# A fixed order of fill groups, smaller adds, and half of the embedding's projection computed ahead of q in an encoder layer

## The chip, the cores and the metric

One NeuronCore of a Trainium2 chip runs the whole kernel. The metric is the device time of one execution in microseconds (us). Three runs of the kernel before gave 1895.80, 1898.79 and 1899.89 us, median 1898.79.

## What is computed

One encoder layer on 256 tokens of width 2048, in float32: a feed-forward half, a mixer of attention heads, a second feed-forward half and a gated input embedding, each between two RMS norms.

```python
def _swiglu(u, w_gate, w_up, w_down):
    return (jax.nn.silu(u @ w_gate) * (u @ w_up)) @ w_down
...
        f = _swiglu(_rmsnorm(h, ffn1_pre_g[i]), ffn1_w_gate[i], ffn1_w_up[i], ffn1_w_down[i])
        h = h + 0.5 * _rmsnorm(f, ffn1_post_g[i])
        m = _mixer(_rmsnorm(h, mix_pre_g[i]), w_qkv[i], na_rpb[i], out_g[i], w_o[i])
        h = h + _rmsnorm(m, mix_post_g[i])
        f = _swiglu(_rmsnorm(h, ffn2_pre_g[i]), ffn2_w_gate[i], ffn2_w_up[i], ffn2_w_down[i])
        h = h + 0.5 * _rmsnorm(f, ffn2_post_g[i])
        g = jax.nn.sigmoid(_rmsnorm(h, ple_pre_g[i]) @ w_ple_gate[i])
        h = h + _rmsnorm(g * (p[i] @ w_ple_proj[i]), ple_post_g[i])
```

The hidden width is 5632, `p` is 256 x 256, `w_ple_proj` 256 x 2048. The embedding's projection `p @ w_ple_proj` depends on no other stage.

## The kernel before

**Numbers in two parts.** Every float32 operand is split into a high part (a cast to fp32r on ACT, ScalarE: `wh`, L81) and a low part (the rest, a subtraction on DVE, VectorE: `wl`, L82). A product of 128 rows is three matmuls of 512 columns: high by high, low by high, high by low (`mac`, L106 to L108; with `low_last`, L99 to L102, in another order). `split` works on two blocks of 128 weight rows at a time and has six buffers for each part, so the splits can run at most six pairs ahead of the matmuls that free them. Weights come by DMA in pieces of 512 KB (`raw`, four buffers, L72), or of 1 MB (`raw_b`, L192).

**The feed-forward half** (`swiglu`) runs over 11 blocks `nb` of 512 hidden columns. Block 0 is computed plainly. Blocks 1 to 10 take gate and up together (`pair_product`): with sums of the token tiles made beforehand (`s1` to `s4`) and sums of weights, seven products of eight row blocks replace eight. In blocks 2 to 10 they are, in order: a11 into bank g0 (copied to g1, L245); a12 into g0; s1 into u0 (copied to u1, L254); s4 into u0; s2 into g1 (copied out, L212); s3 into g1 (copied out, L212); a22 into g1. Each is 24 matmuls. The sums of weights are made in place: `add_rows` (L197) loads rows of w_up on the GpSimd queue with a DMA that adds them to what stands in the buffer, and `add` (L205) adds two buffers on DVE, in pieces of up to four row blocks. Block 1 (`apart`) has another order, in which six of the eight row blocks take part and two are multiplied plainly.

**Fills.** The down product of earlier blocks is cut into groups of 24 matmuls (`down`, for 512 output columns), and `fill()` runs the next one of the list `waiting` at certain places between the seven products. Blocks 3 to 10 have four groups, block 2 has three. The places in blocks 2 to 10 are: before a12; after s1 and the first `add`; after s2; after s3. A `None` in the list is an empty place. Output of a block, transposed (`tr`, L314), is made ready for its own down groups in the next block.

**Between the stages.** At the end of a half the last down groups are scaled and squared (L307, L479), and `residual` makes the factor of the post norm (L301 and L302 on DVE, a power on GpSimd, L303), updates h (L430), transposes it on TensorE (L314) and splits it for the next stage (L318, L320, L321). It is a generator that is run to its end by `list(res)`: after the first half come q and k of the first head group (`halves`), after the second half the embedding. There, all four blocks of 512 columns of `p @ w_ple_proj` are computed (`pp`: 48 matmuls, each block two row blocks, two token tiles, three matmuls), copied out of PSUM (L814) and kept in SBUF, in the place that the second half's sums had; then comes the product of h with `w_ple_gate` (`pg`).

**The order on each engine** is not that of the program text alone: the framework puts each instruction into its engine's queue by priority in program order among those that its own model holds ready. Each engine then works its queue in order.

Of the kernel before, what the change touches and what calls it, by code (L numbers as in the profile page):

```python
# [8 lines left out]
F32 = mybir.dt.float32  # L9
# [6 lines left out]
P = 128  # L16
D = 2048
S = 256
NT = S // P
# [4 lines left out]
NB = 512  # L24
# [10 lines left out]
def encoder_layer(ctx: ExitStack, tc: tile.TileContext, a: dict, out: bass.AP):  # L35
# [6 lines left out]
    nc = tc.nc  # L42
# [22 lines left out]
    def new_raw(name="raw"):  # L65
        return wpool.tile([P, 2, NB], F32, name=name, tag="raw", bufs=4)
# [27 lines left out]
    def mac(acc, xs, parts, first=False, last=False, low_last=False):  # L94


        if low_last:
            for i, ((xh, xl), (wh, wl)) in enumerate(zip(xs, parts)):
                nc.tensor.matmul(acc, xh, wh, start=first and i == 0, stop=False)  # L99
                nc.tensor.matmul(acc, xh, wl, start=False, stop=False)  # L100
            for i, ((xh, xl), (wh, wl)) in enumerate(zip(xs, parts)):
                nc.tensor.matmul(acc, xl, wh, start=False, stop=last and i == len(parts) - 1)  # L102
            return
        for i, ((xh, xl), (wh, wl)) in enumerate(zip(xs, parts)):
            lead, tail = first and i == 0, last and i == len(parts) - 1
            nc.tensor.matmul(acc, xh, wh, start=lead, stop=False, skip_group_check=True)  # L106
            nc.tensor.matmul(acc, xl, wh, start=False, stop=False, skip_group_check=True)  # L107
            nc.tensor.matmul(acc, xh, wl, start=False, stop=tail, skip_group_check=True)  # L108
# [61 lines left out]
    def pair_product(lhs, sums, wa, ca, wb, cb, fill, apart):  # L170

        def bank(name):
            return ps_acc.tile([P, NB], F32, name=f"pair_{name}", tag="acc")

        rq = RQ - 2 * apart
        rows1, rows2 = ([lhs[k] for k in ks[:rq]] for ks in ROWS)
        a11, a12, a22 = of_tile(rows1, 0), of_tile(rows2, 0), of_tile(rows2, 1)
        s1, s2, s3, s4 = (x[:rq] for x in sums)

        def spans(step):  # L180
            for k0, k1 in ((0, KB), (KB, rq)):
                for k in range(k0, k1, step):
                    yield k, min(k + step, k1)

        def weight_rows(w, j, c, k0, k1):
            r0 = ROWS[j][k0] * P
            return w[r0 : r0 + (k1 - k0) * P, c : c + NB].rearrange("(k p) n -> p k n", p=P)

        def blocks(w, j, c, i):
            raw = block_tile(i, [P, RQ, NB], "raw_b")  # L190
            for k0, k1 in spans(KB):
                raw_loads.append(nc.sync.dma_start(raw[:, k0:k1], weight_rows(w, j, c, k0, k1)))  # L192
            return raw

        def add_rows(raw, w, j, c):
            for k0, k1 in spans(2):
                nc.gpsimd.dma_start(raw[:, k0:k1], weight_rows(w, j, c, k0, k1), accum_op=ALU.add)  # L197

        def split_rows(raw):
            return sum((split(raw[:, k : min(k + 2, rq)]) for k in range(0, rq, 2)), [])  # L200

        def add(x, y):
            for k in range(0, rq, 4):
                j = slice(k, min(k + 4, rq))
                nc.vector.tensor_tensor(x[:, j], x[:, j], y[:, j], op=ALU.add)  # L205

        def combine(out_, x, y, op):
            nc.vector.tensor_tensor(out_, x, y, op=op)

        def copied(name, x):  # L210
            t = ffn_pool[0].tile([P, NB], F32, name=name, tag="part", bufs=3)
            nc.scalar.copy(t, x)  # L212
            return t


        def rest(w, c, accs_, i, first=False):
            ks = [x[i] for x in ROWS]
            raw = new_raw()
            rows_ = w[:, c : c + NB].rearrange("(k p) n -> p k n", p=P)
            raw_loads.append(nc.sync.dma_start(raw, rows_[:, ks[0] : ks[1] + 1 : ks[1] - ks[0]]))  # L220
            parts = split(raw)
            for t, acc in accs_:
                mac(acc, of_tile([lhs[k] for k in ks], t), parts, first=first)
        if apart:
            g0, g1, u0, u1 = (bank(x) for x in ("g0", "g1", "u0", "u1"))
            rest(wb, cb, [(1, u1), (0, u0)], RQ - 1, first=True)
            run_later()
            ra1, rb2 = blocks(wa, 0, ca, 0), blocks(wb, 1, cb, 1)
            mac(g1, a11, split_rows(ra1), first=True)
            p1 = copied("p1", g1)  # L230
            add_rows(ra1, wb, 0, cb)
            mac(u0, s4, split_rows(rb2))
            rest(wb, cb, [(1, u1), (0, u0)], RQ - 2)
            fill()
            mac(g0, s1, split_rows(ra1), first=True)
            p5 = copied("p5", g0)
            add(ra1, rb2)
            add_rows(rb2, wb, 0, cb)
            fill()
            ra2 = blocks(wa, 1, ca, 2)  # L240
        else:
            ra1 = blocks(wa, 0, ca, 0)
            g0, g1 = bank("g0"), bank("g1")
            mac(g0, a11, split_rows(ra1), first=True)
            nc.scalar.copy(g1, g0)  # L245
            add_rows(ra1, wb, 0, cb)
            run_later()
            ra2 = blocks(wa, 1, ca, 1)
            fill()
            mac(g0, a12, split_rows(ra2))  # L250
            rb2 = blocks(wb, 1, cb, 2)
            u0, u1 = bank("u0"), bank("u1")
            mac(u0, s1, split_rows(ra1), first=True)
            nc.scalar.copy(u1, u0)  # L254
            add(ra1, rb2)
            fill()
            mac(u0, s4, split_rows(rb2))
            add_rows(rb2, wb, 0, cb)
        mac(g1, s2, split_rows(ra1))
        t4 = ra1 if apart else ra2  # L260
        add(t4, ra2 if apart else ra1)
        u0_ = copied("u0_s", g1)
        if apart:
            combine(u0_, u0_, p5, ALU.subtract)
        combine(u0_, u0, u0_, ALU.subtract)
        fill()
        mac(g1, s3, split_rows(rb2))
        if apart:
            u1_ = p5
            combine(u1_, u1_, g1, ALU.subtract)  # L270
            combine(u1_, u1, u1_, ALU.add)
            mac(g0, a12, split_rows(ra2), first=True)
        else:
            u1_ = copied("u1_s", g1)
            combine(u1_, u1, u1_, ALU.subtract)
            fill()
        mac(g1, a22, split_rows(t4))
        if apart:
            rest(wa, ca, [(0, g0), (1, g1)], RQ - 2)
            rest(wa, ca, [(0, g0), (1, g1)], RQ - 1)  # L280
            combine(p1, g0, p1, ALU.add)
            g0 = p1
            fill()
        block_order[:] = [block_order[i] for i in ((1, 2, 0) if apart else (0, 2, 1))]
        return (g0, g1), (u0_, u1_)
# [172 lines left out]
    def swiglu(pool, f, ssf, res, blocks, rs, sums, w_gate, w_up, w_down, g_post, src):  # L458
# [37 lines left out]
        def downs(nb, b, hid):  # L496
            steps = [] if b not in left else [lambda x=left.pop(b): down(x[0], b, x[1], last=False)]
            return steps + [lambda first=not steps: down(nb, b, hid, first=first)]
# [5 lines left out]
        for nb in range(nbs):  # L504
# [48 lines left out]
            if nb < nbs - 1:  # L553
                now = (0, 1, 2) if nb == 0 else (3, 2) if nb % 2 else (0, 1)
                waiting = sum((downs(nb, b, hid) for b in now), [])
                left.update({b: (nb, hid) for b in range(D // NB) if b not in now})
        for b in (0, 1):
            down(left[b][0], b, left[b][1], last=False, **(dict(pool_=ps_acc, tag="acc") if b else {}))
# [15 lines left out]
                    scaled_out(b, t, acc[t], gp)  # L574


    with tc.tile_pool(name="ffn1", bufs=2) as pool:
        f = pool.tile([P, NT, D], F32, name="f", bufs=1)
        sums_pool[0] = pool
        ssf, u_blocks, u_rs = square_sums(), [], []  # L580
        res = residual(f, ssf, 2.0, u_blocks, u_rs, row_g[:, 1])
        swiglu(
            pool, f, ssf, res, x_blocks, None, [],
            a["ffn1_w_gate"], a["ffn1_w_up"], a["ffn1_w_down"], a["ffn1_post_g"],
            lambda t: a["x"][t * P : (t + 1) * P],
        )
        list(res)
    rs = u_rs

# [194 lines left out]
    mix.close()  # L784


    def embedding_rows():
        p_raw = new_raw("p_raw")
        nc.sync.dma_start(p_raw[:, :, :S], a["pT"].rearrange("(k p) s -> p k s", p=P))
        return split(p_raw[:, :, :S])  # L790

    with tc.tile_pool(name="ffn2", bufs=2) as pool:
        f = f_pool.tile([P, NT, D], F32, name="f")
        ssf, ple_blocks, ple_rs = square_sums(), [], []
# [11 lines left out]
    pp = []  # L806
    for n, pool_, tag in ((RQ, f_pool, "sums_l"), (NT * D // NB - RQ, pool, "pp")):
        y = pool_.tile([P, n, NB], F32, name="pp", tag=tag)
        pp += [y[:, i] for i in range(n)]
    for b in range(D // NB):  # L810
        acc = accs("pp")
        product(acc, p_rows, a["w_ple_proj"], 0, b * NB)
        for t in range(NT):
            nc.scalar.copy(pp[b * NT + t], acc[t])  # L814
# [102 lines left out]
```

## Time and profile before

| | |
|---|---|
| median of three runs | 1898.79 us |
| the profiled execution: its time | 1898.71 us |
| its span | 1896.9 us |
| mean granted TensorE clock | 0.997 |
| busy TensorE / weight loads | 98% / 81% |
| busy DVE / ACT / GpSimd | 80% / 66% / 12% |
| moved by DMA | 424.16 MB, mean 224 GB/s |

The profile is one execution. PE is TensorE, PEld its weight loads, POOL GpSimd, SP the queue that issues most DMAs. A row of a timeline gives start, duration, engine, line, operation, what is written and read, and in brackets the idle time of the engine before it with what ended it. A matmul's duration overlaps the next one's; the distance of starts is what it costs. A row of windows gives, for each engine, busy time and number of instructions in the stretch, then the granted clock, the DMA engines' busy share and their rate. A row of instructions by tile or line gives shortest, median and longest duration in ns, and first and last start.

The stages lie thus in the span: first feed-forward half to 695 us, mixer to 1100, second half to 1784, embedding to the end.

### The profile page before, as it was taken

Reading aid. Unit: us, or ns where it says so; the run is one execution under the profiler, and the core shown is the slowest. Engines: PE = TensorE matmul, PEld = TensorE weight load, DVE = VectorE, ACT = ScalarE, POOL = GpSimd, SP = SyncE. Lnnn points to the kernel's source line nnn. Section 1 sums busy time; section 2 is a strip of 40 time slices with the busy share of each in tenths; the row PEclk is TensorE's granted clock in tenths of the full one; section 3 lists DMA queues with packets and bytes.
Section 4 is the critical chain, followed back from the end, with each engine's and each line's share of the span. In section 5 each row is a group of like instructions: output and inputs, shape, how many; then the busy total and the mean of one; then the engine's idle time right before and its main releaser. Section 6 shows DMA issues by size and latency. Waiting matters only on the chain.

```text
span 1896.9 us, 23645 instructions
## 1 busy us (share of the span) xinstructions
PE 1866.1 (98%) x8492; PEld 1540.7 (81%) x8492; DVE 1525.7 (80%) x1554; ACT 1261.4 (66%) x1592; POOL 221.9 (12%) x189
## 2 busy tenths in 40 slices
PE   8999999999999999999999999999999999999997
PEld 6788888888888878888888888888888888888886
DVE  7898988889888875656665588889988898888765
ACT  7677867777776764544535466778677777767753
POOL 0111112121111100000000001111121111111110
PEclk9999999999999999999999999999999999999999
DMA  9989888898889756454454669898888988897563
GB/s 310 257 247 263 252 226 208 256 279 229 208 237 278 208 177 220 147 197 135 157 189 155 206 205 291 236 260 254 233 204 257 275 233 214 228 277 221 173 221 123
DMA packets 215477, 424.16 MB, mean 224 GB/s; under 512 B 11328, under 2 KB 14400, under 8 KB 214336
## 3 DMA queue, kind: packets, MB, share of 16 engines
q1 hardware_dynamic: 172640, 338.77, 52.5%
q0 software_dynamic: 42720, 83.90, 24.5%
q8 instruction: 66, 1.08, 0.2%
q14 instruction: 51, 0.42, 0.1%
HBM read 418.42 MB, written 4.19 MB: 223 GB/s over the span
## 4 chain that ended last, share of the span: by engine, by line
PE 75%; issue 10%; DMA 6%; DVE 5%; ACT 2%; POOL 1%; SPq 0%; DVEq 0%; POOLq 0%; ACTq 0%
PE pair_g L106 7%; PE pair_g L107 7%; PE pair_g L108 7%; PE down L108 7%; PE down L107 6%; PE down L106 6%; DMA raw_b<-in_ffn_w_up 4%; DVE wl L82 3%; PE pair_u L107 3%; PE pair_u L106 3%; PE pair_u L108 3%; PE v L107 2%; PE v L108 2%; PE v L106 2%; ACT wh L81 1%
## 5 line engine op out<-in xcount | busy, mean ns | idle before, releaser
L82 DVE TENSOR_TENSOR wl<-raw_b,wh 128x1024 fp32r<-128x1024 f32 x546 | 645.2, 1221 | 118.6 <-ACT wh L81 111.7
L81 ACT CAST wh<-raw_b 128x1024 fp32r<-128x1024 f32 x546 | 568.1, 1052 | 252.0 <-DMA raw_b<-in_ffn_w_up 114.6
L82 DVE TENSOR_TENSOR wl<-raw,wh 128x1024 fp32r<-128x1024 f32 (+1 forms) x381 | 459.7, 1219 | 141.4 <-ACT wh L81 129.4
L81 ACT CAST wh<-raw 128x1024 fp32r<-128x1024 f32 (+1 forms) x381 | 396.9, 1051 | 237.4 <-PE k L107 39.6
L197 POOL DMA_DIRECT2D raw_b<-in_ffn_w_up x156 | 190.7, 1274 | 1003.9 <-DVE wl L82 867.3
L108 PE MATMUL down<-wl,hid_h 128*128 128x512 f32 x640 | 251.0, 392 | 6.5 <-DVE wl L82 6.3
L106 PE MATMUL down<-wh,hid_h 128*128 128x512 f32 x640 | 251.0, 392 | 0.0
L107 PE MATMUL down<-wh,hid_l 128*128 128x512 f32 x640 | 249.2, 389 | 0.0
L108 PE MATMUL pair_g<-wl,u_h 128*128 128x512 f32 x484 | 188.3, 390 | 0.7 <-DVE wl L82 0.7
L106 PE MATMUL pair_g<-wh,u_h 128*128 128x512 f32 x484 | 188.5, 389 | 0.0
L107 PE MATMUL pair_g<-wh,u_l 128*128 128x512 f32 x484 | 188.3, 389 | 0.0
L205 DVE TENSOR_TENSOR raw_b<-raw_b 128x2048 f32<-128x2048 f32 x80 | 178.6, 2233 | 0.7
L108 PEld LDWEIGHTS down<-wl,hid_h 128*128 128x128 f32 x640 | 120.1, 188 | 37.5 <-DVE wl L82 12.9
L107 PEld LDWEIGHTS down<-wh,hid_l 128*128 128x128 f32 x640 | 120.2, 188 | 24.5
L106 PEld LDWEIGHTS down<-wh,hid_h 128*128 128x128 f32 x640 | 120.2, 188 | 23.8
L106 PE MATMUL pair_g<-wh,sums_h 128*128 128x512 f32 x324 | 126.2, 389 | 1.7 <-ACT u_s L212 1.7
L108 PE MATMUL pair_g<-wl,sums_h 128*128 128x512 f32 x324 | 126.1, 389 | 0.0
L107 PE MATMUL pair_g<-wh,sums_l 128*128 128x512 f32 x324 | 126.0, 389 | 0.0
L106 PE MATMUL pair_u<-wh,sums_h 128*128 128x512 f32 x300 | 116.7, 389 | 0.0
L107 PE MATMUL pair_u<-wh,sums_l 128*128 128x512 f32 x300 | 116.7, 389 | 0.0
L108 PE MATMUL pair_u<-wl,sums_h 128*128 128x512 f32 x300 | 116.7, 389 | 0.0
L108 PEld LDWEIGHTS pair_g<-wl,u_h 128*128 128x128 f32 x484 | 90.9, 188 | 20.0 <-DVE wl L82 1.2
(227 smaller groups left out, 2893.7 us busy)
## 6 DMA issues: line engine op xcount, KB each, us to landing
raw<-in_ffn_w_down SPq DMA_DIRECT2D x176, 512.0 KB, 9.0
raw_b<-in_ffn_w_up POOLq DMA_DIRECT2D x156, 512.0 KB, 10.1
raw_b<-in_ffn_w_gate SPq DMA_DIRECT2D x76, 1024.0 KB, 7.2
raw<-in_w_qkv SPq DMA_DIRECT2D x96, 512.0 KB, 4.8
raw_b<-in_ffn_w_up SPq DMA_DIRECT2D x38, 1024.0 KB, 7.4
raw<-in_w_o SPq DMA_DIRECT2D x32, 512.0 KB, 4.9
raw<-in_w_ple_gate SPq DMA_DIRECT2D x32, 512.0 KB, 5.1
raw<-in_ffn_w_up SPq DMA_DIRECT2D x20, 512.0 KB, 4.2
```

What stands on the lines that cost most here:

```text
L81: nc.scalar.copy(wh[:, :n], raw),
L82: nc.vector.tensor_tensor(wl[:, :n], raw, wh[:, :n].bitcast(F32), op=ALU.subtract),
L106: nc.tensor.matmul(acc, xh, wh, start=lead, stop=False, skip_group_check=True)
L107: nc.tensor.matmul(acc, xl, wh, start=False, stop=False, skip_group_check=True)
L108: nc.tensor.matmul(acc, xh, wl, start=False, stop=tail, skip_group_check=True)
L197: nc.gpsimd.dma_start(raw[:, k0:k1], weight_rows(w, j, c, k0, k1), accum_op=ALU.add)
L205: nc.vector.tensor_tensor(x[:, j], x[:, j], y[:, j], op=ALU.add)
```

## The change

Four edits:

1. In block 1, `add` works in pieces of two row blocks instead of four.
2. In blocks 2 to 10 the third fill moves from after s2 to between s4 and s2, and the fourth from after s3 to after s2. After s3 there is none.
3. A `None` goes in as second entry of the list that block 2 uses: its three groups stand at the first, third and fourth place.
4. After the first feed-forward half, ahead of `list(res)`, p is loaded and split and two of the four blocks of the projection are computed, copied to SBUF (a buffer of the half's weights, then free) and stored to a buffer in HBM by four DMAs on the GpSimd queue. At the end p is loaded and split again, four DMAs on SP's queue load the stored blocks, and only the other two blocks are computed.

```diff
         def add(x, y):
-            for k in range(0, rq, 4):
-                j = slice(k, min(k + 4, rq))
+            n = 2 if apart else 4
+            for k in range(0, rq, n):
+                j = slice(k, min(k + n, rq))
                 nc.vector.tensor_tensor(x[:, j], x[:, j], y[:, j], op=ALU.add)
...
             fill()
             mac(u0, s4, split_rows(rb2))
             add_rows(rb2, wb, 0, cb)
+            fill()
         mac(g1, s2, split_rows(ra1))
...
             u1_ = copied("u1_s", g1)
             combine(u1_, u1, u1_, ALU.subtract)
-            fill()
         mac(g1, a22, split_rows(t4))
...
                 waiting = sum((downs(nb, b, hid) for b in now), [])
+                if nb == 1: waiting.insert(1, None)
...
+    p_kept = dram.tile([P, NT * 2, NB], F32, name="p_kept")
...
+        p_rows, p_out = embedding_rows(), block_tile(2, [P, 2 * NT, NB], "pp_s")
+        for b in range(2):
+            acc = [ps_acc.tile([P, NB], F32, name=f"pp{t}", tag="acc") for t in range(NT)]
+            product(acc, p_rows, a["w_ple_proj"], 0, b * NB, jobs=False)
+            for t in range(NT):
+                nc.scalar.copy(p_out[:, b * NT + t], acc[t])
+                nc.gpsimd.dma_start(p_kept[:, b * NT + t], p_out[:, b * NT + t])
         list(res)
...
-    for b in range(D // NB):
+    for i in range(2 * NT):
+        nc.sync.dma_start(pp[i], p_kept[:, i])
+    for b in range(2, D // NB):
         acc = accs("pp")
         product(acc, p_rows, a["w_ple_proj"], 0, b * NB)
```

The function `embedding_rows` (one DMA and one split of p) moves up unchanged.

More of the change, by code (lines that the diff above doesn't have):

```diff
@@ L574, in swiglu, with embedding_rows @@
                     scaled_out(b, t, acc[t], gp)
+    def embedding_rows():
+        p_raw = new_raw("p_raw")
+        nc.sync.dma_start(p_raw[:, :, :S], a["pT"].rearrange("(k p) s -> p k s", p=P))
+        return split(p_raw[:, :, :S])
+    p_kept = dram.tile([P, NT * 2, NB], F32, name="p_kept")
     with tc.tile_pool(name="ffn1", bufs=2) as pool:
@@ L784, in encoder_layer @@
     mix.close()
[L787 to L790, printed above, removed]
     with tc.tile_pool(name="ffn2", bufs=2) as pool:
```

## The prediction

> **What bounds the kernel now.** I read the page's table of engines first, then TensorE's waits, then windows cut at the feed-forward blocks, then the timelines of the few gaps, last the windows at the two places between which work moves.
>
> ```profile
> span 1896.9 us, 23645 instructions
> ...
> PE 1866.1 (98%) x8492; PEld 1540.7 (81%) x8492; DVE 1525.7 (80%) x1554; ACT 1261.4 (66%) x1592; POOL 221.9 (12%) x189
> ```
>
> TensorE is busy 98% of the span. An edit of order can win only in the few gaps, and it can lose wherever it opens one. The waits (us in total, times, longest) name the main one inside the feed-forward halves:
>
> ```profile
> PE down L108 <- DVE wl L82: 6.3, 11, 1.3
> ```
>
> Here are three whole blocks of the first half as windows, cut where the first down group begins: block 2, with three down groups, then two blocks with four. Columns are the window, its length, busy times of PE, PEld, DVE, ACT, POOL, clock, DMA share, GB/s.
>
> ```profile
> 119.93:176.00 56.07, 55.59 (x251) 45.87 (x250) 51.87 (x45) 42.81 (x51) 9.17 (x9) 1.00 0.90 243
> ...
> 237.28:299.09 61.81, 61.02 (x276) 50.31 (x273) 54.36 (x47) 45.12 (x53) 9.74 (x8) 1.00 0.89 243
> 544.50:605.32 60.82, 60.82 (x275) 50.29 (x273) 54.45 (x47) 45.08 (x53) 9.77 (x8) 1.00 0.88 237
> ```
>
> The third block has no gap at all: 60.82 us for 264 long matmuls and 8 short transposes, 0.227 us a matmul, so a group of 24 (a down group, or one of the seven products of a pair) takes 5.44 us. The second block loses 61.81 - 60.82 = 0.99 us, all in one place, the second down group:
>
> ```profile
> 255.28 0.39 PE L107 MATMUL down<-wh,hid_l 128*128 128x512 f32 x1
> 256.45 0.50 PE L108 MATMUL down<-wl,hid_h 128*128 128x512 f32 x1 [0.79 <-DVE wl L82]
> ```
>
> ```profile
> 252.98 2.28 DVE L205 TENSOR_TENSOR raw_b<-raw_b 128x2048 f32<-128x2048 f32 x1
> 255.18 1.22 DVE L82 TENSOR_TENSOR wl<-raw,wh 128x1024 fp32r<-128x1024 f32 x1
> ```
>
> DVE does 2.28 us of L205 ahead of the low part that the matmul needs. That is the ceiling of the reordering: with 6.3 us in 11 such waits (0.6 each), and not in every block, about 0.5 us a block.
>
> **Fills in blocks 2 to 10.** The third down group now stands between s4 and s2, the fourth between s2 and s3. No group stands between s3 and a22 any more, and a22 adds into the bank (g1) that ScalarE must first copy after s3. The trace shows this neighbourhood already: block 2 has only three groups, so its fourth place is empty.
>
> ```profile
> 163.55 0.39 PE L106 MATMUL pair_g<-wh,u_h 128*128 128x512 f32 x1
> 163.77 0.39 PE L107 MATMUL pair_g<-wh,u_l 128*128 128x512 f32 x1
> 164.01 0.49 PE L314 MATMUL tr<-ident,u_s 128*128 128x128 f32 x3
> 164.97 0.50 PE L108 MATMUL pair_g<-wl,u_h 128*128 128x512 f32 x1 [0.47 <-DVE wl L82]
> ```
>
> ```profile
> 164.47 0.58 ACT L212 COPY u_s<-pair_g 128x512 f32<-128x512 f32 x1
> ```
>
> s3 ends before 163.55. While the copy runs (164.47 to 165.05) PE takes two matmuls of the next a11 and three transposes, then stands 0.47 us for a low part. The whole block costs 56.07 + 5.44 = 61.51, 0.69 over the block without a gap. So the direct step costs 0 (filled from the next block) to 0.69 us. What comes off: DVE, ahead by one more light group at that point, can have the low part earlier; and what PE loses there is partly a loss of the second group's wait, since the accumulating loads run on meanwhile. I take +0.1 us a block for the 16 blocks 3 to 10 of both halves: **+1.6** (bounds -0.5 x 16 = -8, if the wait of the second group goes and nothing comes, and +0.69 x 16 = +11).
>
> In block 2 the empty place moves from the fourth to the second call: s4 follows s1 directly, into the bank (u0) that ScalarE copies in between. That copy is of the form of the 0.58 us row above; with at most one weight cast ahead of it on ACT (1.05, row below) the step costs 0 to 1.7. I take 0.9, twice: **+1.8**. The direct step s3 to a22 was in block 2 before, so nothing changes there.
>
> **Smaller adds in block 1.** Two pieces of an add become three:
>
> ```profile
> 79.31 0.50 PE L108 MATMUL down<-wl,hid_h 128*128 128x512 f32 x1 [1.33 <-DVE wl L82]
> ```
>
> ```profile
> 74.70 3.42 DVE L205 TENSOR_TENSOR raw_b<-raw_b 128x2048 f32<-128x2048 f32 x2
> ```
>
> The group's low part waits behind 3.42 us of add; between smaller pieces it may go first. Bounds 0 and -1.33; I take **-0.8** for the first half alone.
>
> **What the move out of the end frees, and what it costs at q.** Half of the projection is two weight loads of 512 KB, two splits, 24 matmuls and four copies:
>
> ```profile
> L106 PE MATMUL pp<-wh x16: 389/389/499, 1784.5 to 1798.3; 128*128 128x512 f32 x16
> ...
> L814 ACT COPY pp<-pp x8: 563/592/619, 1790.6 to 1799.4; 128x512 f32<-128x512 f32 x8
> ```
>
> ```profile
> L82 DVE TENSOR_TENSOR wl<-p_raw,wh x1: 692/692/692, 1777.5 to 1777.5; 128x512 fp32r<-128x512 f32 x1
> ```
>
> ```profile
> L82 DVE TENSOR_TENSOR wl<-raw,wh 128x1024 fp32r<-128x1024 f32 (+1 forms) x381 | 459.7, 1219 | 141.4 <-ACT wh L81 129.4
> L81 ACT CAST wh<-raw 128x1024 fp32r<-128x1024 f32 (+1 forms) x381 | 396.9, 1051 | 237.4 <-PE k L107 39.6
> ```
>
> ```profile
> L439 POOL DMA_DIRECT2D h_kept<-h x2: 593/612/630, 1099.3 to 1110.2; - x2
> ```
>
> L106 is a third of the 48 matmuls. Ahead of q come 24 x 0.227 = 5.44 us of PE, 0.69 + 2 x 1.22 = 3.13 us of DVE (p is split a second time), about 2 x 1.05 + 4 x 0.59 = 4.5 us of ACT and four stores on POOL's queue, nearest row L439, 0.61 each. L303's power for the second token tile is issued on the same queue; I take the 0 to 2.4 us as hidden, because the power is due before the copies that the stores wait for. At the end the same 5.44 us of PE, 2.44 of DVE and 4.5 of ACT go. SP swaps two loads of 512 KB for four of 256 KB: 1 MB either way, into a tile that nothing has used since the last pair product.
>
> ```profile
> 698.80 0.80 PE L99 MATMUL q<-wh,u_h 128*128 128x512 f32 x1 [3.26 <-ACT u_h L320]
> 699.39 0.63 PE L100 MATMUL q<-wl,u_h 128*128 128x512 f32 x1
> 699.82 0.63 PE L99 MATMUL q<-wh,u_h 128*128 128x512 f32 x1
> ```
>
> ```profile
> 694.00:698.00 4.00, 1.54 (x11) 1.13 (x10) 4.00 (x6) 2.96 (x7) 0.00 (x0) 1.00 0.82 258
> 698.00:702.00 4.00, 3.20 (x8) 2.59 (x9) 3.68 (x7) 3.56 (x8) 1.37 (x1) 0.57 0.71 233
> ...
> 1796.00:1800.00 4.00, 4.00 (x24) 3.35 (x23) 4.00 (x8) 4.00 (x11) 2.66 (x1) 1.00 0.51 142
> ```
>
> Ahead of q PE stands 3.26 us, and then runs at a clock of 0.57 in the window from 698: starts 0.43 us apart instead of 0.227, some 8 matmuls to the end of that window, 8 x 0.2 = 1.6. The 5.44 us of moved matmuls thus displace 3.26 + 1.6 = 4.9 us; by PE alone the place costs +0.5. But DVE is full there (4.00 of 4, then 3.68), and the 3.13 us more of it can hardly be hidden; so between +0.5 and +3.1, I take **+2.3**. At the end, PE alone gives -5.44. But DVE and ACT are full (4.00 and 4.00), and DVE is rid of 2.44 only: PE then reaches the gate's product early and waits for its splits. Between -5.4 and -2.4, I take **-3.0**.
>
> **The sum**: 1.6 + 1.8 - 0.8 + 2.3 - 3.0 = +1.9. The profiled execution took 1898.71 us (span 1896.9 and 1.8 around it), practically the median of 1898.79. Forecast 1900.6 us. A measurement of this kernel can tell about 0.2%, 3.8 us, from no change, so this counts as none.
>
> **A rule weighed against the trace.** The accumulating loads (L197) decide when s1 and the second group's split can run. Three windows of them: the first three of block 3 (starts, time to landing, and the load on SP ahead of them), the same of block 4, and the time to landing of those from 257.5 on, when SP loads little:
>
> ```profile
> L197 POOL DMA_DIRECT2D raw_b<-in_ffn_w_up x3: 1204/1214/1323, 165.3 to 169.0; - x3
> ```
>
> ```profile
> DMA to landing us min/median/max: 10.0/13.2/14.9
> ```
>
> ```profile
> 158.64 0.92 SPq L192 DMA_DIRECT2D raw_b<-in_ffn_w_gate  x2
> ```
>
> ```profile
> L197 POOL DMA_DIRECT2D raw_b<-in_ffn_w_up x3: 1204/1214/1222, 226.9 to 229.7; - x3
> ```
>
> ```profile
> DMA to landing us min/median/max: 11.1/13.7/16.3
> ```
>
> ```profile
> 216.48 0.92 SPq L192 DMA_DIRECT2D raw_b<-in_ffn_w_gate  x2
> ```
>
> ```profile
> DMA to landing us min/median/max: 5.9/8.2/9.6
> ```
>
> With s3 one group later, the next block's 2 MB of gate rows (L192), whose buffer s3 frees, start one group nearer to the accumulates. In block 3 they stood 6.7 us ahead of them, in block 4 10.4, and the nearer ones cost nothing (10.0 against 11.1). The Trainium skill, "DMA: Bandwidth & Descriptors", "Issuing engines are not separate DMA queues", has transfers from all issuing engines interleave on the same 16 engines. By that rule the accumulates would land later; by the rows of block 3 they don't, and my sum goes by the rows.
>
> **The rivals.**
> (1) Faster: PE alone is the bound, DVE and ACT move their work into free time. Then the two places give 0.5 - 5.4 = -4.9 instead of -0.7, and the direct step is filled from the next block, which turns +1.6 into -0.3 x 16 = -4.8 as half of the second group's waits go: 1898.7 - 4.9 - 4.8 + 1.8 - 0.8 = 1890.0, or 1894.9 if the waits stay. For it: PE never stood at the end, where DVE was as full. Against it: it didn't stand there because it had the 10.9 us of the projection to do, and DVE's 4.00 of 4 leaves no free time to move work into.
> (2) Slower: the direct step from s3 to a22 costs what block 2 shows, 0.69 us in each of 16 blocks, +11 instead of +1.6: 1898.7 + 1.9 + 9.4 = 1910.0. It decides from a net 0.22 us a block on, (3.8 - 1.9) / 16 + 0.1. For it: block 2 of the trace is exactly this order. Against it: in block 2 DVE came out of s4 and s2 without a group between, which now stands there.
> (3) The accumulates land later by half the difference between block 4's rows and those from 257.5 on, (11.1 - 5.9) / 2 = 2.6 us, all of it behind the second group: 16 x 2.6 = 42, 1942. Only this would be the rule above at work; block 3 speaks against it.
> (4) The moved projection is put behind the transposes of h by whatever orders the queue, and fills nothing: PE +5.4 and -3 to -5.4 there, 1898.7 + 2.6 + 0 to 2.4 = 1901 to 1904.
>
> **How the numbers follow.** Forecast 0.40, (1) 0.24, (2) 0.28, (3) 0.03, (4) 0.05. Faster by over 0.2%: 0.24, rival (1). Slower: (2), (3) and a part of (4), 0.33. Within: 0.43. The range leaves out (3), and the far halves of (1) and (2): 1892 to 1909; the forecast's own range is 1896 to 1903.
>
> **What would show it.** Right: between the first half and q no idle row of 3 us and clock 1.00, but a PE wait of 1 to 3 us on DVE or ACT soon after; at the end a PE wait of about 2 us before or in the gate's product; blocks 3 to 9 between 60.9 and 61.8 us; in block 2 a wait of about 1 us between pair_u and pair_u. Wrong, to the fast side: blocks of 60.8 and an end that is 5 us shorter. Wrong, to the slow side: in each block an idle PE between the last pair_g of s3 and the first of a22, released by ACT u_s L212 or DVE wl L82, of 0.4 us and more; or accumulates that land later than 16.3 us.

## The result, and the profile after

| | before | after |
|---|---|---|
| median of 22 runs each, us | 1898.24 | 1894.67 |
| lowest to highest, us | 1895.61 to 1899.89 | 1892.42 to 1897.43 |
| ratio of after to before | | 0.9984, 95% interval 0.9977 to 0.9990 |
| the profiled execution: time / span, us | 1898.71 / 1896.9 | 1897.36 / 1895.6 |

By the ratio, the change makes the kernel faster by 3.0 us (1.9 to 4.4; the two medians differ by 3.6). That is less than the 3.8 us that the prediction counted as no change, but it goes the other way than the forecast of +1.9. The profiled execution after took nearly the longest time of its runs, so lengths of stages are compared below over many profiles, not from one pair. Two more rounds of the same kernel gave 0.9989 (0.9980 to 0.9998) and 0.9991 (0.9982 to 0.9999).

The page's head and table of engines of the kernel after:

```profile
span 1895.6 us, 23701 instructions
...
PE 1869.9 (99%) x8492; PEld 1541.5 (81%) x8492; DVE 1535.3 (81%) x1559; ACT 1263.7 (67%) x1593; POOL 218.9 (12%) x193
```

TensorE's waits after (total, times, longest). Lines are one further down than before (L82 is unchanged; L430 became L431, L318 became L319), and from the end's copies on 13 further (L814 became L827):

```profile
PE down L108 <- DVE wl L82: 3.2, 5, 1.6
PE tr L315 <- DVE y_g L319: 1.8, 2, 1.4
...
PE pg L99 <- ACT pp L827: 0.6, 1, 0.6
```

The second group's wait halved, from 6.3 us in 11 to 3.2 in 5. The wait of 3.3 us ahead of q is gone as a row; one of 1.37 on DVE stands in its place.

**The blocks.** Windows of after, cut as those of before: block 2, a block that still has a wait, and one of the many that have none.

```profile
119.91:177.31 57.40, 56.20 (x252) 45.74 (x250) 52.44 (x45) 42.69 (x51) 9.31 (x9) 1.00 0.90 239
238.86:300.58 61.72, 61.35 (x276) 50.32 (x274) 54.72 (x47) 45.16 (x53) 10.12 (x9) 1.00 0.89 241
422.76:483.86 61.10, 61.07 (x276) 50.39 (x274) 55.08 (x47) 45.48 (x53) 9.42 (x8) 1.00 0.88 240
```

Before, blocks of a full set of groups took anything from 60.82 to 61.91 us; after, eight of these sixteen take 61.09 or 61.10. What nearly every block now pays is the direct step from s3 to a22 (TensorE's timeline, block 3, then its weight loads):

```profile
226.84 0.39 PE L106 MATMUL pair_g<-wh,u_h 128*128 128x512 f32 x1
227.07 0.39 PE L107 MATMUL pair_g<-wh,u_l 128*128 128x512 f32 x1
227.30 0.49 PE L315 MATMUL tr<-ident,u_s 128*128 128x128 f32 x3
227.83 0.50 PE L108 MATMUL pair_g<-wl,u_h 128*128 128x512 f32 x1
```

```profile
227.82 0.19 PEld L108 LDWEIGHTS pair_g<-wl,u_h 128*128 128x128 f32 x1 [0.27 <-DVE wl L82]
```

Between the starts at 227.07 and 227.83 lie 0.76 us; a matmul takes 0.23 of it and three transposes some 0.11 each (their distance of starts), so 0.2 is lost. The next start comes 0.33 us later, which loses 0.1 more. TensorE's rows show no wait here, but the bracket of the weight load does: it waits for DVE's low part, and not for ScalarE's copy of the bank. The step thus costs some 0.3 us, by which 61.09 also lies over the 60.82 of the block without a gap. Block 2 has the new wait between s1 and s4, filled with four matmuls of the next down group:

```profile
136.10 0.39 PE L108 MATMUL pair_u<-wl,sums_h 128*128 128x512 f32 x1
137.42 0.50 PE L106 MATMUL down<-wh,hid_h 128*128 128x512 f32 x1 [0.93 <-ACT wh L81]
...
138.86 0.50 PE L106 MATMUL pair_u<-wh,sums_h 128*128 128x512 f32 x1 [0.24 <-ACT pair_u L255]
```

Over all profiles of this study the lengths of the parts can be averaged: 8 with the old order of fills, 10 with the new (two groups of kernels, whatever else they change; each number from windows cut in the same places; mean, in brackets lowest and highest, us).

| part | old order | new order | difference | predicted |
|---|---|---|---|---|
| block 1, first half | 62.62 (60.54 to 64.62) | 61.56 (61.10 to 62.21) | -1.1 | -0.8 |
| block 1, second half | 59.37 (59.37 to 59.38) | 59.38 (59.37 to 59.41) | 0.0 | 0 |
| block 2, both halves | 112.06 (111.28 to 112.72) | 114.19 (113.81 to 115.80) | +2.1 | +1.8 |
| blocks 3 to 10, both halves | 979.74 (977.38 to 981.20) | 978.50 (977.66 to 980.35) | -1.2 | +1.6 |

In block 1 the wait that got shorter is not the one that the smaller adds were meant for. That one, in the second down group, was 1.1 to 1.4 us in six of the eight old profiles and missing in two; it is 1.3 to 2.2 in all ten new ones. Another, 16 us later, for a copy on ScalarE, was 0.87 to 2.55 us in the old profiles and is at most 0.63 in the new (before, then after):

```profile
95.86 0.50 PE L106 MATMUL pair_g<-wh,sums_h 128*128 128x512 f32 x1 [1.74 <-ACT u_s L212]
```

```profile
95.84 0.50 PE L106 MATMUL pair_g<-wh,sums_h 128*128 128x512 f32 x1 [0.63 <-ACT u_s L213]
```

No run shows by what way the smaller adds shorten it.

**Ahead of q.** The windows of after from 694, and TensorE's timeline there:

```profile
694.00:698.00 4.00, 4.00 (x20) 3.30 (x19) 4.00 (x7) 2.98 (x7) 0.49 (x1) 1.00 0.68 219
698.00:702.00 4.00, 2.78 (x17) 2.18 (x15) 3.54 (x6) 3.81 (x9) 2.74 (x4) 1.00 0.85 235
702.00:706.00 4.00, 3.82 (x22) 2.96 (x22) 3.94 (x8) 3.17 (x5) 0.54 (x1) 1.00 0.95 338
```

```profile
699.75 1.03 PE L315 MATMUL tr<-ident,h 128*128 128x128 f32 x8
702.15 1.25 PE L315 MATMUL tr<-ident,h 128*128 128x128 f32 x8 [1.37 <-DVE y_g L319]
703.43 0.50 PE L99 MATMUL q<-wh,u_h 128*128 128x512 f32 x1
```

The clock stays at 1.00, where before it fell to 0.57: TensorE no longer stands 3.26 us. But the 24 matmuls of the projection now stand ahead of the transposes of h (694.30 to 699.75), and the chain from the transposes to q, which made the gap, follows them: rival (4) had feared them behind the transposes, and ahead of them they fill only a part of it. The prediction let the 5.44 us of matmuls displace 4.9 us; the stretch from the first half's last down matmul to v is 3.2 us longer (below), so they displace 2.2. DVE's and GpSimd's timelines show what the second set of transposes waits for:

```profile
698.40 1.22 DVE L82 TENSOR_TENSOR wl<-raw,wh 128x1024 fp32r<-128x1024 f32 x1
700.09 1.41 DVE L431 SCALAR_TENSOR_TENSOR h<-f,r,h 128x512 f32<-128x512 f32 x2 [0.46 <-POOL r L304]
701.42 1.28 DVE L319 TENSOR_TENSOR y_g<-tr,row_g 128x512 f32<-128x512 f32 x2
```

```profile
698.58 1.47 POOL L304 TENSOR_TENSOR r<-m,mhalf 128x1 f32<-128x1 f32 x1 [0.44 <-DVE m L303]
```

The transposes end at 700.78, but y_g, which empties their bank, starts at 701.42: ahead of it in DVE's queue stand two updates of h, and those stand 0.46 us for the power.

**At the end** TensorE stands once, 0.64 us, and not for DVE. The two windows of after, and the wait:

```profile
1792.00:1796.00 4.00, 3.37 (x16) 2.46 (x15) 3.87 (x8) 4.00 (x11) 1.14 (x1) 1.00 0.76 260
1796.00:1800.00 4.00, 3.97 (x25) 2.98 (x24) 3.58 (x6) 4.00 (x9) 0.38 (x1) 1.00 0.51 166
```

```profile
1795.13 0.50 PE L99 MATMUL pg<-wh,u_h 128*128 128x512 f32 x1 [0.64 <-ACT pp L827]
```

Before, it stood there once too, for the same kind of copy on ScalarE, so rival (1) was not right that TensorE never stood at the end:

```profile
1791.25 0.50 PE L106 MATMUL pp<-wh 128*128 128x512 f32 x1 [1.04 <-ACT pp L814]
```

The accumulating loads of w_up (L197) land as before (then 5.8, 10.1 and 17.1 us from issue):

```profile
DMA to landing us min/median/max: 5.8/10.5/16.1
```

The stages as lengths on TensorE, start to start, in all profiles that can be compared: from the last down matmul of the first half to v (the move into the place ahead of q), 52.53 us on average without it (51.26 to 53.95, six kernels) and 55.56 with it as the change has it (55.37 to 55.80, seven): **+3.0**. From the last down matmul of the second half to the last matmul of the gate's product, 102.8 without the move (102.43 to 103.21, four) and 97.7 with it (97.46 to 97.97, ten): **-5.1**. In the two profiled executions alone it is +3.2 and -5.7. With the table's -0.2 for the order, the stages give -2.3 (-2.7 by the two executions); the times gave -3.0, -2.1 and -1.7.

### The profile page after: what moved, and what is told of

Read it like the earlier page. It is cut to its first block, busy times and chain, and to the rows that moved or that the text cites. A ratio compares the mean times of both kernels' runs of the same rounds, so it can differ in the third digit from the quotient of the medians.

```text
span 1895.6 us, 23701 instructions
## 1 busy us (share of the span) xinstructions
PE 1869.9 (99%) x8492; PEld 1541.5 (81%) x8492; DVE 1535.3 (81%) x1559; ACT 1263.7 (67%) x1593; POOL 218.9 (12%) x193
## 4 chain that ended last, share of the span: by engine, by line
PE 79%; issue 10%; DMA 4%; DVE 2%; ACT 1%; POOL 1%; DVEq 0%; POOLq 0%; ACTq 0%; SPq 0%
PE pair_g L108 8%; PE pair_g L106 8%; PE pair_g L107 8%; PE down L108 7%; PE down L106 7%; PE down L107 7%; DMA raw_b<-in_ffn_w_up 3%; PE pair_u L106 3%; PE pair_u L107 3%; PE pair_u L108 3%; PE v L108 2%; PE v L106 2%; PE v L107 2%; PE tr L315 1%; PE q L107 1%
## 5 line engine op out<-in xcount | busy, mean ns | idle before, releaser
L82 DVE TENSOR_TENSOR wl<-raw_b,wh 128x1024 fp32r<-128x1024 f32 x546 | 649.9, 1222 | 118.2 <-ACT wh L81 103.5
L82 DVE TENSOR_TENSOR wl<-raw,wh 128x1024 fp32r<-128x1024 f32 (+1 forms) x381 | 460.2, 1220 | 137.1 <-ACT wh L81 123.0
L197 POOL DMA_DIRECT2D raw_b<-in_ffn_w_up x156 | 190.6, 1258 | 1001.5 <-DVE wl L82 865.8
L206 DVE TENSOR_TENSOR raw_b<-raw_b 128x2048 f32<-128x2048 f32 (+1 forms) x84 | 178.7, 2134 | 0.7
## 6 DMA issues: line engine op xcount, KB each, us to landing
raw_b<-in_ffn_w_up POOLq DMA_DIRECT2D x156, 512.0 KB, 10.5
```

What stands on the lines that cost most here:

```text
L82: nc.vector.tensor_tensor(wl[:, :n], raw, wh[:, :n].bitcast(F32), op=ALU.subtract),
```

## The experiments

My theory after the result: the prediction's order of the sum holds but for the end, where TensorE was the bound and DVE, though busy all the time, was ahead of it. Rivals: the new order of fills carries the gain; or the place ahead of q costs less than it seems.

### The parts alone

The fourth edit alone (edits 1 to 3 undone), and edits 1 to 3 alone:

```diff
-            n = 2 if apart else 4
-            for k in range(0, rq, n):
+            for k in range(0, rq, 4):
...
-            fill()
         mac(g1, s2, split_rows(ra1))
...
+            fill()
         mac(g1, a22, split_rows(t4))
...
-                if nb == 1: waiting.insert(1, None)
```

> Only edit 4, the projection's half moved; fills and adds as before. Theory A (the whole gain comes from the move: at the end PE is rid of its 5.4 us and more, ahead of q it pays about 3): -2.5 us against the kernel before, -1.5 to -4. Theory B (the gain comes from the order of the fills, the move is worth nothing, as the prediction had it: +2.3 - 3.0): -0.7 us, 0 to -1.5.

Measured 1895.99 us, ratio 0.9999 (0.9990 to 1.0008).

> Only edits 1 to 3: smaller adds in block 1, the order of the fills, the empty place in block 2; no move. Theory A: 0 us, -1 to +1, since what the second group's wait gives back is spent on the direct step from s3 to a22. Theory B: -2 to -4 us. The prediction had +2.6.

Measured 1896.94 us, ratio 1.0000 (0.9991 to 1.0009). The whole, again:

> The changed kernel itself once more, beside the versions made from it. Theory A (end -5.6, ahead of q +3.1, order of the fills 0): -2.5 us, -1 to -4.

Measured 1894.15 us, ratio 0.9989 (0.9980 to 0.9998). Neither part shows the whole's gain by its time alone, so both were run again beside the whole:

> The fourth edit alone, once more, beside the other edits alone and the whole. By the lengths of the stages it costs 3.1 us ahead of q and gives 5.6 at the end: ratio 0.9987. The times of the first round gave 0.9999 (0.9990 to 1.0008). If the stages are right, this round lies below 0.9995; if the fourth edit alone is worth nothing and only works with the new order, again at 1.000.

> The first three edits alone, once more. By the lengths of the two halves the order is worth nothing (means within 0.3 us): 1.0000. The prediction's terms for the same edits are +2.6 us, 1.0014. If the order carries the whole's gain, 0.9985.

> The changed kernel, beside its parts on one chip. By the stages -2.5 us, 0.9987; the two rounds before gave 0.9984 and 0.9989. The parts and the whole are compared by the sum of their differences.

Measured 0.9994 (0.9984 to 1.0004), 0.9998 (0.9989 to 1.0006) and 0.9991 (0.9982 to 0.9999). The order is worth nothing in both rounds, as the lengths say and against the prediction's +2.6. The fourth edit gave 0.9999 and 0.9994, on average -0.7 us, where the lengths give -2.1. A ratio of 0.9989, which the lengths would make, is just outside the first interval and within the second; whether the edit is worth more together with the new order is below what these rounds can tell, and stays open.

### The two places one by one

Only the front (computed and stored ahead of q, and all four blocks still computed at the end), and only the end (two blocks there are loaded from other rows, so half of the projection is left out):

```diff
+        p_rows, p_out = embedding_rows(), block_tile(2, [P, 2 * NT, NB], "pp_s")
+        for b in range(2):
...
         list(res)
```

```diff
-    for b in range(D // NB):
+    for i in range(2 * NT):
+        nc.sync.dma_start(pp[i], a["ffn1_w_gate"][i * P : (i + 1) * P, :NB])
+    for b in range(2, D // NB):
```

> The kernel before with half of the projection computed, copied and stored ahead of q in addition; the end still computes all four blocks, so 24 matmuls are done twice. It measures the cost at q by itself. Theory A (in the new queue the 24 matmuls stand ahead of the transposes of h, so the chain from h to q is waited for all the same): +3.2 us, +2.5 to +4.5. Rival (DVE's 3.1 us more decide, as the prediction had it): +2.3, +0.5 to +3.1. If PE alone decided and the gap were filled: +0.5.

Measured 1900.18 us, ratio 1.0021 (1.0012 to 1.0029): +4.0 us.

> The kernel before with only two blocks of the projection computed at the end; the other two are loaded from rows of another weight, so the output leaves out half of the projection and nothing is computed ahead of q. It measures the gain at the end by itself. Theory A (PE alone decides there): -5.4 to -6 us. The prediction's step (DVE, rid of 2.44 us only, decides): -3.0, -2.4 to -3.5.

Measured 1890.49 us, ratio 0.9970 (0.9960 to 0.9980): -5.7 us, nearly twice the forecast's term and all of the 5.44 us of TensorE. The end is one of the two places where the prediction went wrong; the other is the order of the fills.

### At the end: TensorE, DVE, or both

Three kernels relieve the two engines separately. In the first, two blocks at the end have no low part of the weights (2.44 us of DVE less, the same number of matmuls):

```diff
+            parts = [(h, h) for h, _ in split(load_rows(a["w_ple_proj"], 0, 2, b * NB), low=False)]
```

> The kernel before, where two of the four blocks at the end take the weight's high part in place of the low one: these low parts are left out, 2.4 us of DVE, with all matmuls, casts and copies kept. Theory A (PE decides at the end, DVE's full windows are work done ahead): from the second half's last down matmul to the gate's last one 103.2 us as before, 102.7 to 103.3. The prediction's step (DVE decides): 100.8.

The second is the changed kernel with two subtractions of 128x1024 put back on DVE at the end (`y_kept` is one of the two buffers in which the projection is kept); the third is the kernel before without two blocks' matmuls, but with their splits:

```diff
+    for i in range(2):
+        idle = wpool.tile([P, 2, NB], F32R, name="wl", bufs=6)
+        nc.vector.tensor_tensor(idle, y_kept[:, 2 * i : 2 * i + 2], y_kept[:, 2 * i : 2 * i + 2], op=ALU.subtract)
```

```diff
+    for b in range(2):
+        split(load_rows(a["w_ple_proj"], 0, 2, b * NB))
+        run_later()
+    for b in range(2, D // NB):
```

> The changed kernel with two additional subtractions of 128x1024 on DVE at the end, where the two splits were that the change took away; their result is not read. Theory A (PE alone decides at the end): from the second half's last down matmul to the gate's last one 97.5 us as in the changed kernel, at most 98.3. The prediction's step (DVE decides there): 2.4 us more, 99.9.

> The kernel before, with TensorE alone relieved at the end: two of the four blocks of the embedding's projection keep their loads and their splits on ACT and DVE, but not their 24 matmuls and copies; four loads of another weight's rows fill their places, so half of the projection is left out. Length from the last down group to the last matmul of the gate's product: 103.2 us in the kernel before, 97.7 where DVE was rid of 2.44 us too. If DVE was the bound there, as the prediction's step had it, nothing comes of it: 102.6 to 103.2. If DVE was full but some way ahead, the gain is what it was ahead by, and end_dve_more puts that at 2.3 us: 100.9. If DVE does not matter at all, 97.7.

One time of each: 1897.09 us (before: 1896.55), 1900.35 (before: 1897.18) and 1895.84 (before: 1896.91). The reading is the window from the last down matmul to the last matmul of the gate's product, in one execution of each kernel; its first number is the length, then busy PE, PEld and DVE. Before, then without DVE's 2.44 us alone:

```profile
1783.49:1886.70 103.21, 102.14 (x466) 84.12 (x464) 66.51 (x82) 56.80 (x89) 9.67 (x4) 1.00 0.54 174
```

```profile
1781.21:1885.11 103.90, 102.09 (x466) 84.25 (x464) 64.72 (x80) 56.80 (x89) 3.67 (x4) 1.00 0.52 168
```

Without TensorE's 5.44 us alone, in both forms (splits kept; subtractions put back):

```profile
1781.33:1883.63 102.30, 98.97 (x442) 79.38 (x440) 66.99 (x82) 55.53 (x85) 8.69 (x4) 1.00 0.55 176
```

```profile
1787.36:1888.28 100.92, 98.39 (x442) 79.32 (x440) 66.61 (x82) 53.71 (x83) 5.14 (x4) 1.00 0.51 168
```

Without both, the change:

```profile
1787.78:1885.30 97.52, 96.85 (x441) 79.58 (x440) 64.26 (x80) 53.17 (x83) 4.08 (x4) 1.00 0.53 173
```

So DVE's relief alone gives nothing (+0.7), TensorE's alone 0.9 to 2.3, both together 5.7. The four kernels with the old end lie between 102.43 and 103.21 us, so each of these numbers has some 0.8 us of scatter. The +0.7 holds a pause of 1.33 us ahead of the transposes of h for which the profile names no releaser:

```profile
1790.25 0.63 PE L317 MATMUL tr<-ident,h 128*128 128x128 f32 x4 [1.33 <-issue]
```

But the row of before already says that little could come of DVE alone: TensorE was busy 102.14 of the 103.21 us. In the kernel before DVE was not the bound; had TensorE alone been relieved, it would have become the bound at once. The timeline of TensorE in the kernel that keeps the splits shows it, with rows that the change does not have:

```profile
1783.94 0.50 PE L108 MATMUL pp<-wl,wh 128*128 128x512 f32 x1 [0.41 <-DVE wl L82]
...
1790.09 0.49 PE L100 MATMUL pg<-wl,u_h 128*128 128x512 f32 x1 [0.39 <-DVE wl L82]
...
1796.27 1.25 PE L314 MATMUL tr<-ident,h 128*128 128x128 f32 x8 [0.32 <-DVE y_g L318]
```

If DVE were ahead by some s, the gain with both would be 2.44 + s, that is 3.3 to 4.7 with s of 0.9 to 2.3. It was 5.1 to 5.7. The rest, 0.4 to 2.4 us, stays open: by the windows ACT is rid of 3.6 us in the change and of 1.3 in the kernel that keeps the splits, and the queues are laid out anew in each.

### Ahead of q: DVE's amount, or the order

The residual put ahead of the projection, in the changed kernel and with the old order of fills:

```diff
+        list(res)
         p_rows, p_out = embedding_rows(), block_tile(2, [P, 2 * NT, NB], "pp_s")
...
-        list(res)
```

> The changed kernel with the whole of the residual placed ahead of the projection in the program, so that the transposes of h have the higher priority. Theory A (what is paid ahead of q is paid because the 24 matmuls stand ahead of the transposes, so that the chain from h to q runs after them): the transposes go first, the matmuls fill the chain's time, the stretch from the first half's end to v falls from 55.5 to about 53, and the whole stands at -4.5 to -5.5 us against the kernel before. Rival (DVE's additional 3.1 us decide there): the stretch stays at 55 or more, the whole at -2.5.

> The same placing with the fills, the adds and block 2's list as before the change. Theory A: as res_first within 1 us, -4 to -5.5 us, since the order of the fills is worth nothing. If the order is worth something it stands 1 to 3 us above res_first.

Measured 1893.39 us, 0.9986 (0.9977 to 0.9994), and 1896.20, 0.9992 (0.9981 to 1.0002). Then the low parts of the moved half left out (3.1 us less on DVE), in both places, and computed by GpSimd:

```diff
-        return split(p_raw[:, :, :S])
+        return split(p_raw[:, :, :S], low)
...
-            product(acc, p_rows, a["w_ple_proj"], 0, b * NB, jobs=False)
+            parts = [(h, h) for h, _ in split(load_rows(a["w_ple_proj"], 0, 2, b * NB), low=False)]
```

> The changed kernel, where the 24 matmuls ahead of q take the high part in place of the low one, of p and of the weight: the low parts of p and of two blocks of the projection are left out, 3.1 us of DVE there, with all matmuls, casts and copies kept. Theory D (DVE decides ahead of q): the stretch from the first half's last down matmul to v falls from 55.5 us by 2 to 3, to 52.5 to 53.5. Theory Q (the place of the matmuls ahead of the transposes decides): 55 to 55.5.

> The same, with the residual ahead of the projection in the program, so that both are taken away; the same low parts are left out. Theory D: 52.5 us as front_no_low or a little less, since PE then has 5.4 us more and gaps and slow clock of about 5 us less than before the change, 52.3. If neither DVE nor the place decides: 55.2, as with the residual first alone.

> A whole kernel: the change with the residual first, and with the three low parts ahead of q made on GpSimd, which has nothing else to do there but one power. Theory D: the stretch falls to about 53 us and the whole stands at -5 to -6 us against the kernel before, unless the GpSimd subtractions take over 5 us each or hold up the power. Theory Q: as the residual first alone, -2.7 us.

Measured 1896.62 and 1895.21, one time of each (before: 1896.55), and for GpSimd 1899.31, ratio 1.0012 (1.0004 to 1.0021). The windows from the last down matmul to v, one execution of each; the change, the residual first, the change without low parts, the residual first without low parts, the residual first with GpSimd:

```profile
694.08:749.60 55.52, 53.68 (x250) 43.98 (x249) 40.92 (x54) 31.91 (x52) 5.82 (x7) 1.00 0.76 249
```

```profile
691.44:746.69 55.25, 53.69 (x250) 43.83 (x249) 40.81 (x53) 32.09 (x52) 5.32 (x7) 1.00 0.76 253
```

```profile
692.66:750.33 57.67, 54.52 (x250) 45.45 (x249) 38.72 (x51) 32.07 (x52) 4.93 (x7) 0.97 0.70 230
```

```profile
693.79:748.13 54.34, 53.05 (x251) 43.88 (x249) 38.74 (x51) 31.92 (x52) 4.93 (x7) 1.00 0.73 245
```

```profile
692.45:753.20 60.75, 56.04 (x251) 46.19 (x249) 43.28 (x55) 32.55 (x52) 6.44 (x8) 0.94 0.71 231
```

My expectations for the residual first failed in both kernels: the wait ahead of q goes, but others come later, and the stretch is shorter by 0.3 us only. TensorE's two largest waits there:

```profile
700.70 0.52 PE L315 MATMUL tr<-ident,h 128*128 128x128 f32 x3 [0.72 <-issue]
...
717.77 0.50 PE L100 MATMUL k<-wl,u_h 128*128 128x512 f32 x1 [0.76 <-DVE wl L82]
```

And less work on DVE, with the residual behind, made the stretch longer by 2.1 us, not shorter. DVE's timeline without low parts, and TensorE's, say why:

```profile
697.99 2.08 DVE L434 SCALAR_TENSOR_TENSOR h<-f,r,h 128x512 f32<-128x512 f32 x3 [0.69 <-POOL r L307]
699.99 0.74 DVE L434 SCALAR_TENSOR_TENSOR h<-fg,r,h 128x512 f32<-128x512 f32 x1
700.65 1.22 DVE L85 TENSOR_TENSOR wl<-raw,wh 128x1024 fp32r<-128x1024 f32 x1
701.78 1.28 DVE L322 TENSOR_TENSOR y_g<-tr,row_g 128x512 f32<-128x512 f32 x2
```

```profile
698.34 1.03 PE L318 MATMUL tr<-ident,h 128*128 128x128 f32 x8
702.52 1.97 PE L318 MATMUL tr<-ident,h 128*128 128x128 f32 x8 [3.15 <-DVE y_g L322]
```

The transposes end at 699.37, and y_g stands behind four updates of h and a split: the framework has laid DVE's queue another way, and TensorE stands 3.15 us. With the residual first, where no such thing happens, the 3.1 us of DVE are worth 55.25 - 54.34 = 0.9, by one execution of each.

In the last kernel GpSimd's two large subtractions and DVE's updates of h take place side by side (GpSimd's timeline, then DVE's):

```profile
688.34 5.62 POOL L82 TENSOR_TENSOR wl<-raw,wh 128x1024 fp32r<-128x1024 f32 x2
```

```profile
691.64 2.87 DVE L431 SCALAR_TENSOR_TENSOR h<-f,r,h 128x512 f32<-128x512 f32 x1
694.43 0.74 DVE L431 SCALAR_TENSOR_TENSOR h<-fg,r,h 128x512 f32<-128x512 f32 x1
```

An update of 0.74 us takes 2.87 beside a GpSimd subtraction, and ends half a microsecond after it: relieving DVE this way cost it more than it gave, and the expected -5 to -6 us came out as +2.3. No version that computes the whole layer is better than the change by more than the intervals can tell.

## Why the prediction was wrong, point by point

- **What bounds the kernel**: right. TensorE was 98% busy, is 99% now, and the gain is what its gaps and its moved work allow.
- **Smaller adds in block 1, -0.8; block 2's empty place, +1.8**: measured -1.1 (with a scatter of 4 us in the old kernels, so only the sign is likely) and +2.1. The reason given for the adds was wrong and the sign right by luck: the wait that they were to shorten, 1.33 us, is 1.59 in the profile after, and the gain lies in another wait. The wait in block 2 is where it was put, between s1 and s4, 0.93 us.
- **Blocks 3 to 10, +1.6**: measured -1.2, by the scatter of the 18 profiles some 1 us either way. This is the largest miss, 2.8 us, and a term that was mis-sized, not a wrong mechanism. The step to correct is "I take +0.1 us a block": both sides of it are there, but their balance is the other. The shortest of blocks 3 to 9 rose from 60.73 to 61.07 us over all profiles, which is the direct step, some 0.3 us a block and not up to 0.69. What the blocks take above that shortest one fell more, from 0.52 on average to 0.11. The second group's wait shows it: 2.2 to 6.6 us in all in the eight profiles with the old order, 1.4 to 3.2 in the ten with the new. So a block costs 0.07 us less and not 0.1 more.
- **Ahead of q, +2.3**: measured +3.0 (+4.0 by the time of the front alone), at its bound of +3.1. The mechanism was half right: TensorE's stand and its low clock go, and part of the 5.44 us isn't hidden. But the matmuls displace only 2.2 to 2.4 us of the 4.9 that the prediction gave them, and the reason given, DVE's 3.13 us more, is worth 0.9 where it could be taken away alone. That the rest goes with where the moved matmuls and the steps of the chain from the transposes to q stand in their queues is argued from the timelines; the kernels with the residual first did not show it. An order of TensorE's queue that fills too little was rival (4), with a chance of 0.05.
- **The end, -3.0**: this is the step whose mechanism failed, in these words: "DVE and ACT are full (4.00 and 4.00), and DVE is rid of 2.44 only: PE then reaches the gate's product early and waits for its splits." Measured -5.1 to -5.7. A window in which DVE is full says that it never pauses; it does not say that anybody waits for it, and the profile of before had no wait on DVE there: TensorE was busy 102.14 of the 103.21 us and stood once, for a copy on ScalarE, while DVE was busy 66.51. The 2.44 us that DVE was rid of were needed (without them the gain is 0.9 to 2.3), and with them nothing waited for DVE. The expected wait of about 2 us in the gate's product was 0.64, on ACT.
- **The rule on the accumulates, rival (3)**: not borne out; they land at 10.5 us in the median, before at 10.1, at most 16.1.
- **The rivals**: (1) has the size of the end right (-5.4), but not its reason: TensorE's relief alone gives 0.9 to 2.3. It is wrong ahead of q (+0.5) and for the blocks (-4.8). That its 1890 to 1894.9 us holds the time is luck, since this round's time before was 0.5 us below the one it starts from; as a difference it had -3.8 to -8.7 and -3.0 came. (2), 0.69 us a block, did not come.
- **The signs**: of those for being right, the clock of 1.00 and a wait of 1 to 3 us on DVE ahead of q came (1.37), and the wait of about 1 us in block 2 (0.93). Of those for being wrong to the fast side, the end that is 5 us shorter came, and blocks of 60.8 did not (61.09).
- **The sum**: -0.2 for the order instead of +2.6, +3.0 instead of +2.3, -5.1 instead of -3.0, in all -2.3 instead of +1.9. Of these 4.2 us, blocks 3 to 10 make 2.8 and the end 2.1; the other terms take 0.7 of it back.

## What to carry to other kernels

A window in which an engine is full is no bound: look for the rows in which another engine waits for it, and, where there are none, ask how far ahead of its users it is. Here, taking the same work off two engines gave all of TensorE's share, and taking it off either alone gave little. Work moved into an engine's gap fills it only in part where the queues put it ahead of the chain that made the gap. Putting the start of the chain first was not enough here (0.3 us), since each engine of the chain has a queue of its own in which its step can stand behind other work. An order of work that takes waits away can give it back as a small fixed cost: average over many blocks and many profiles before giving it a sign.

## What the runs showed of the hardware

GpSimd and DVE can stop each other. The update of h takes 0.74 us alone and 2.87 beside a GpSimd subtraction of 2.83. The Trainium skill, "SBUF — State Buffer", section "SBUF: two separate sides", calls the pair of ports that the two share an exclusive lock and not a bandwidth split, held for the whole instruction, also between a DVE operation with two SBUF inputs and a GpSimd operation that reads SBUF; the trace agrees, with 2.87 us for 0.74 of work. GpSimd's subtraction itself took 2.83 us, where DVE's takes 1.22. Between the first half and q, the power of one column took 0.97 to 1.47 us where DVE was busy with two-input operations, and 0.56 or 0.57 where it was not.
